# A residual-add RMSNorm on one core: static addresses on SyncE, gamma in 16 chunks on the bulk queue, no block barrier

## The chip, the cores and the metric

The kernel runs on one core of a Trainium2 chip. The metric is the device time of one execution in microseconds (us); lower is better. "Span" is the time from the first to the last instruction in a profile; the device time was 1.7 to 2.1 us longer than the span in every run, and verdicts rest on the device time.

## The reference

```python
batch, seq, dim = 32, 2048, 2048          # x, residual: float32; gamma: float32[2048]; eps 1e-6
z = x + residual
rms = np.sqrt(np.mean(z ** 2, axis=-1, keepdims=True) + eps)
return (z / rms * gamma).astype(np.float32)
```

There are 65,536 rows of 8 KB. Each row of x and of the residual is read once and each output row written once, 1610.6 MB in all.

## The kernel before

The rows are cut into 74 tiles: 128 partitions x 3 rows, then x 5, then 72 tiles of 128 x 7 rows (7.34 MB for each of x, residual and output). SyncE issues every bulk transfer. VectorE adds the residual into x (L179), ScalarE squares and sums (L230) and takes the root (L238), VectorE scales by the reciprocal and gamma (L184). SyncE's turn for tile i stores tile i-1, loads residual i+1 and loads x i+1:

```python
def sp_turn(sp, t):
    i = t.i
    t.wait(sp, "done", -1)
    inc(sp.dma_start(out=t.dram(o_f, o_full, -1), in_=z[(i - 1) % 2][:, : sizes[i - 1], :]), "s_out", i - 1)
    ...
    t.wait(sp, "add_a")
    load_r(sp, t, 1)
    t.wait(sp, "s_out", -1)
    ...
    load_x(sp, t, 1)
```

Turns 3 to 70 stand in a hardware loop whose addresses are worked out in registers:

```python
@block.sync
def _(sp):
    load_x(sp, Turn(0))
    load_r(sp, Turn(0))
    load_r(sp, Turn(1))
    load_x(sp, Turn(1))
    for i in range(1, LO):
        sp_turn(sp, Turn(i))
    with sp.Fori(0, 2 * n_iter, 2) as it:
        for i in range(LO, LO + 2):
            sp_turn(sp, Turn(i, it))
    ...
```

Gamma is read four times, into partitions 0, 32, 64 and 96, by ScalarE's queue; VectorE then copies it to all partitions of a PSUM tile with one shuffle:

```python
@block.scalar
def _(s):
    s.wait_ge(tail_ev["add"], 1)
    for q in range(4):
        s.dma_start(out=r_area[32 * q : 32 * q + 1, R, :], in_=gamma.partition_broadcast(1)).then_inc(g_in, U)
```

Of the kernel before, what the change touches and what calls it, by code (L numbers as in the profile page):

```python
# [9 lines left out]
def kernel(  # L10
# [17 lines left out]
    nc = tc.nc  # L28
    P = nc.NUM_PARTITIONS
# [4 lines left out]
    x_f = x.flatten_outer_dims()  # L34
    r_f = residual.flatten_outer_dims()
    o_f = out.flatten_outer_dims()

    n_rows, D = x_f.shape
    R = 7
    STEP = 4  # L40
    U = 16
    lead = [3, 5]
    n_full = (n_rows // P - sum(lead)) // R
    sizes = lead + [R] * n_full
    starts = [0]
# [3 lines left out]
    n_tiles = len(sizes)  # L49
    last = n_tiles - 1  # L50

    LO = 3
    n_iter = (last - 1 - LO) // 2
    HI = LO + 2 * n_iter
    assert n_iter >= 1

    def rows(t, i):
        k = sizes[i]
        return t[starts[i] : starts[i] + P * k, :].rearrange("(p r) m -> p r m", r=k)

    def full(t):
        return t[starts[2] :, :].rearrange("(n p r) m -> n p r m", p=P, r=R)

    x_full, r_full, o_full = full(x_f), full(r_f), full(o_f)

    inv_d = 1.0 / float(D)

    def sb(name, shape):
        return ctx.enter_context(nc.sbuf_tensor(name, shape, fp32))

    def ps(name, shape):
        return ctx.enter_context(nc.psum_tensor(name, shape, fp32))
# [3 lines left out]
    def sem(name):  # L76
        sems.append(ctx.enter_context(nc.semaphore(name)))
        return sems[-1]
# [3 lines left out]
    z = [sb(f"z{p}", [P, R, D]) for p in range(2)]  # L82
    r_area = sb("r_area", [P, R + STEP, D])
# [8 lines left out]
    gamma_tile = ps("gamma_tile", [P, D])  # L92
# [5 lines left out]
    g_in = sem("g_in")  # L98
    dve = sem("dve_own")
    act = sem("act_own")  # L100
    s_tail = sem("s_tail")
    tail_ev = {k: sem(f"tail_{k}") for k in ("add", "rms", "done")}


# [2 lines left out]
    def entry(i):  # L107
        if i == 0:
            return R + STEP - sizes[0]
        return 0 if i % 2 else STEP  # L110
# [7 lines left out]
    class Turn:  # L118
# [10 lines left out]
        def wait(self, eng, kind, d=0):  # L129
            eng.wait_ge(ev[kind][(self.i + d) % 2], self.at(d))  # L130

        def dram(self, t, t_full, d):
            if self.it is None:
                return rows(t, self.i + d)
            return t_full[self.it + (self.i + d - 2)]

    def inc(ins, kind, i):
        return ins.then_inc(ev[kind][i % 2], U)


    def load_x(sp, t, d=0):
        i = t.i + d
        inc(sp.dma_start(out=z[i % 2][:, : sizes[i], :], in_=t.dram(x_f, x_full, d)), "x_in", i)  # L143

    def load_r(sp, t, d=0):
        i = t.i + d
        e = entry(i)
        inc(
            sp.dma_start(out=r_area[:, e : e + sizes[i], :], in_=t.dram(r_f, r_full, d)),
            "r_in",  # L150
            i,
        )

    def sp_turn(sp, t):
        i = t.i
        t.wait(sp, "done", -1)
        inc(
            sp.dma_start(out=t.dram(o_f, o_full, -1), in_=z[(i - 1) % 2][:, : sizes[i - 1], :]),  # L158
            "s_out",
            i - 1,  # L160
        )
        if t.it is None and i == last:
            return
        t.wait(sp, "add_a")
        load_r(sp, t, 1)
        t.wait(sp, "s_out", -1)
        if t.it is None and i + 1 == last:
            for k, (a, b) in enumerate(tail):
                sp.dma_start(  # L169
                    out=z[last % 2][:, a:b, :], in_=rows(x_f, last)[:, a:b, :]  # L170
                ).then_inc(x_tail[k], U)
        else:
            load_x(sp, t, 1)


    def add(v, i, a, b):
        e = entry(i)
        s = z[i % 2][:, a:b, :]
        return v.tensor_add(out=s, in0=s, in1=r_area[:, e + a : e + b, :])  # L179

    def scale(v, i, a, b, rs, c=0):
        for g in range(a, b):
            s = z[i % 2][:, g, :]
            ins = v.scalar_tensor_tensor(  # L184
                out=s,
                in0=s,
                scalar=rs[:, c + g - a : c + g - a + 1],
                in1=gamma_tile[:, :],
                op0=mult,
                op1=mult,  # L190
            )
        return ins

    def dve_turn(v, t, own):
        i, p = t.i, t.p
        t.wait(v, "x_in")
        t.wait(v, "r_in")
        (a0, b0), (a1, b1) = parts(i)
        inc(add(v, i, a0, b0), "add_a", i)
        inc(add(v, i, a1, b1), "add_b", i)  # L200
        for h, (a, b) in enumerate(parts(i)):
            n = b - a
            t.wait(v, "rms_a" if h == 0 else "rms_b")
            v.reciprocal(out=rstd[p][h][:, :n], in_=rms[p][h][:, :n]).then_inc(dve, U)  # L204
            v.wait_ge(dve, own(i, h))
            ins = scale(v, i, a, b, rstd[p][h])
        inc(ins, "done", i)
# [42 lines left out]
                i,  # L250
            )

    block_ctx = nc.Block()
    block = block_ctx.__enter__()

    @block.sync
    def _(sp):
        load_x(sp, Turn(0))
        load_r(sp, Turn(0))
        load_r(sp, Turn(1))  # L260
        load_x(sp, Turn(1))
        for i in range(1, LO):
            sp_turn(sp, Turn(i))
        with sp.Fori(0, 2 * n_iter, 2) as it:
            for i in range(LO, LO + 2):
                sp_turn(sp, Turn(i, it))
        for i in range(HI, n_tiles):
            sp_turn(sp, Turn(i))
        for k, (a, b) in enumerate(tail):
            sp.wait_ge(tail_ev["done"], k + 1)  # L270
            sp.dma_start(
                out=rows(o_f, last)[:, a:b, :], in_=z[last % 2][:, a:b, :]
            ).then_inc(s_tail, U)
        sp.wait_ge(s_tail, U * len(tail))
        sp.wait_ge(ev["s_out"][(last - 1) % 2], ((last - 1) // 2 + 1) * U)

    @block.vector
    def _(v):
        row = R
        v.memset(eps_tile[:, :], float(eps))  # L280
        v.memset(r_area[:, row, :], 0.0).then_inc(tail_ev["add"], 1)  # L281
        v.wait_ge(g_in, 4 * U)
        v.stream_shuffle(gamma_tile[:, :], r_area[:, row, :], [0] * 32)  # L283
        for i in range(LO):
            dve_turn(v, Turn(i), lambda i, h: (2 * i + h + 1) * U)
        with v.Fori(0, 2 * n_iter, 2) as it:
            for i in range(LO, LO + 2):
                dve_turn(v, Turn(i, it), lambda i, h: it * (2 * U) + (2 * i + h + 1) * U)
        for i in range(HI, last):
            dve_turn(v, Turn(i), lambda i, h: (2 * i + h + 1) * U)  # L290
        base = 2 * last * U
        t = Turn(last)
        t.wait(v, "r_in")

        def tail_scale(k):
            a, b = tail[k]
            v.wait_ge(tail_ev["rms"], k + 1)
            v.reciprocal(out=tail_rstd[:, a:b], in_=tail_rms[:, a:b]).then_inc(dve, U)  # L298
            v.wait_ge(dve, base + (k + 1) * U)
            scale(v, last, a, b, tail_rstd, a).then_inc(tail_ev["done"], 1)  # L300

        for k, (a, b) in enumerate(tail):
            v.wait_ge(x_tail[k], U)
            add(v, last, a, b).then_inc(tail_ev["add"], 1)
            if k:
                tail_scale(k - 1)
        tail_scale(len(tail) - 1)

    @block.scalar
    def _(s):  # L310

        s.wait_ge(tail_ev["add"], 1)
        for q in range(4):
            s.dma_start(
                out=r_area[32 * q : 32 * q + 1, R, :], in_=gamma.partition_broadcast(1)
            ).then_inc(g_in, U)
        chain = Chain(s, act)
        for i in range(LO):
            act_turn(s, Turn(i), chain)
        with s.Fori(0, 2 * n_iter, 2) as it:  # L320
            n = chain.n
            chain.base = it * R
            for i in range(LO, LO + 2):
                act_turn(s, Turn(i, it), chain)
            assert chain.n - n == 2 * R
        chain.base = None
        chain.n = n + 2 * R * n_iter
        for i in range(HI, last):
            act_turn(s, Turn(i), chain)
        for k, (a, b) in enumerate(tail):  # L330
            chain.wait()
            s.wait_ge(tail_ev["add"], k + 2)
            act_part(
                s, chain, z[last % 2], a, b, tail_ssq[:, a:b], tail_rms[:, a:b]
            ).then_inc(tail_ev["rms"], 1)

    block_ctx.__exit__(None, None, None)

    ids = [a.num for a in sems]
    assert ids == list(range(ids[0], ids[0] + len(ids)))  # L340
    nc.gpsimd.sem_clear(range(ids[0], ids[-1] + 1))
# [35 lines left out]
```

## Time and profile before

| | before |
|---|---|
| device time, median of 3, later 4 runs | 3727.06, later 3727.15 us (3726.29 to 3727.42) |
| span of the profiled run | 3724.2 us |
| VectorE, ScalarE busy | 62%, 29% |
| DMA rate over the span | 432 GB/s |

The prediction below shows the lines of the page and of both edges. Two more readings: The first is the timeline around gamma (columns: start, duration, engine, line, operation, out<-in with shapes, count; in brackets the idle time before and what ended it):

```profile
14.70 2.29 DVE L283 STREAM_SHUFFLE gamma_tile<-r_area 128x2048 f32<-128x2048 f32 x1
19.36 4.43 DVE L179 TENSOR_TENSOR z<-z,r_area 128x4096 f32<-128x4096 f32 x1 [2.38 <-DMA r_area<-in_residual_dram]
```

The shuffle is over before the first residual lands, so gamma costs VectorE no waiting.

The second is the DMA view of the steady part alone, 200 to 3600 us (packets, MB and rate; then each queue with its packets, MB and share of 16 engines' time):

```profile
DMA packets 28936, 1474.96 MB, mean 434 GB/s; under 512 B 3215, under 2 KB 3215, under 8 KB 3215
...
q1 hardware_dynamic: 28936, 1474.96, 100.2%
```

Only the bulk queue q1 moves anything here. No gamma packet (queue q10) and no instruction packet (queue q14) falls into this window.

**A reading that needs the packet records.** The trace has the start, duration, size and queue of each DMA packet, but not its engine. A transfer over 16 engines ends with sixteen packets of 4 bytes, one from each engine. Sorting their ends for each transfer gives how far each engine is behind the middle one; I call the largest of these the **lag**.

### The profile page before, as it was taken

The numbers are of one execution on the slowest core, as the hardware profiler recorded it, in microseconds if no ns is written. First come the engines' busy times: TensorE is split into PE (matmuls) and PEld (weight loads), VectorE is DVE, ScalarE is ACT, GpSimd is POOL, SyncE is SP. The second block draws the span as 40 slices with busy tenths as digits, with TensorE's granted clock in tenths as the row PEclk, the third lists the DMA queues.
The fourth block names the chain that finished last, engine by engine and source line by source line (L and its number), as shares of the span: only waits on it lengthen the run. The fifth ranks groups of instructions, "written<-read, shape, count | busy, mean of one in ns | idle before, by whom it ended". The sixth has DMA issues, their size and how long they took to land.

```text
span 3724.2 us, 4147 instructions
## 1 busy us (share of the span) xinstructions
DVE 2302.6 (62%) x816; ACT 1072.4 (29%) x1176; POOL 0.2 (0%) x4
## 2 busy tenths in 40 slices
DVE  4666565566665566665566665566665566665566
ACT  2333322233322233322233322233322233322233
POOL 0000000000000000000000000000000000000000
DMA  9999999999999999999999999999999999999999
GB/s 420 430 434 434 434 434 434 434 434 434 434 434 434 434 434 434 433 434 434 434 434 434 434 434 434 435 434 434 435 434 434 434 435 434 434 434 434 434 434 400
DMA packets 32842, 1610.68 MB, mean 432 GB/s; under 512 B 3652, under 2 KB 3652, under 8 KB 3652
## 3 DMA queue, kind: packets, MB, share of 16 engines
q1 hardware_dynamic: 32832, 1610.63, 100.0%
q10 hardware_dynamic: 8, 0.03, 0.0%
q14 instruction: 2, 0.02, 0.0%
HBM read 1073.77 MB, written 536.87 MB: 432 GB/s over the span
## 4 chain that ended last, share of the span: by engine, by line
DMA 66%; DVE 22%; issue 9%; ACT 2%; SPq 0%; DVEq 0%; ACTq 0%
DMA out_dram<-z 33%; DMA z<-in_x_dram 33%; DVE z L179 15%; DVE z L184 7%; ACT sq_junk L230 1%; DMA r_area<-in_residual_dram 0%; ACT rms L238 0%; DVE rstd L204 0%; SPq L158 0%; DVEq L130 0%; ACTq L218 0%; ACTq L130 0%; DVE tail_rstd L298 0%; SPq L143 0%; SPq L169 0%
## 5 line engine op out<-in xcount | busy, mean ns | idle before, releaser
L179 DVE TENSOR_TENSOR z<-z,r_area 128x8192 f32<-128x8192 f32 (+2 forms) x150 | 1109.4, 7436 | 1257.3 <-DMA z<-in_x_dram 1227.2
L230 ACT ACTIVATE sq_junk<-z 128x2048 f32<-128x2048 f32 x512 | 963.4, 1882 | 2613.5 <-DVE z L179 2602.1
L184 DVE SCALAR_TENSOR_TENSOR z<-z,rstd,gamma_tile 128x2048 f32<-128x2048 f32 x505 | 1153.5, 2343 | 5.2
L204 DVE RECIPROCAL rstd<-rms 128x4 f32<-128x4 f32 (+2 forms) x146 | 25.2, 173 | 130.9 <-ACT rms L238 130.9
L230 ACT ACTIVATION_READ_ACCUMULATOR sq_junk<-z 128x1 f32 x512 | 95.4, 186 | 0.0
L238 ACT ACTIVATE rms<-ssq,eps_tile 128x4 f32<-128x4 f32 (+2 forms) x146 | 43.3, 297 | 13.4
L184 DVE SCALAR_TENSOR_TENSOR z<-z,tail_rstd,gamma_tile 128x2048 f32<-128x2048 f32 x7 | 16.2, 2345 | 0.1
L283 DVE LOAD_MASK_SELECT gamma_tile<-r_area x1 | 0.0, 14 | 11.5 <-DMA r_area<-in_gamma_dram 11.5
L230 ACT ACT_TABLE_LOAD x1 | 1.3, 1283 | 4.7 <-issue 4.7
L283 DVE STREAM_SHUFFLE gamma_tile<-r_area 128x2048 f32<-128x2048 f32 x1 | 2.3, 2290 | 0.0
L281 DVE MEMSET r_area<- 128x2048 f32 x1 | 1.8, 1765 | 0.4 <-issue 0.4
L238 ACT ACT_TABLE_LOAD x1 | 1.3, 1283 | 0.1
L238 ACT ACTIVATE tail_rms<-tail_ssq,eps_tile 128x2 f32<-128x2 f32 (+1 forms) x4 | 1.2, 295 | 0.1
L280 DVE MEMSET eps_tile<- 128x1 f32 x1 | 0.1, 59 | 1.0 <-SPq L80 1.0
L298 DVE RECIPROCAL tail_rstd<-tail_rms 128x2 f32<-128x2 f32 (+1 forms) x4 | 0.6, 157 | 0.0
L358 POOL MEMSET const-bfloat16-1.0<- 128x1 bf16 x1 | 0.1, 102 | 0.0
L358 POOL MEMSET const-uint8-127<- 128x1 uint8 x1 | 0.1, 102 | 0.0
L358 POOL MEMSET const-float32-0.0<- 128x1 f32 x1 | 0.1, 99 | 0.2 <-issue 0.2
L358 POOL MEMSET const-float32-1.0<- 128x1 f32 x1 | 0.1, 99 | 0.0
## 6 DMA issues: line engine op xcount, KB each, us to landing
r_area<-in_residual_dram SPq DMA_DIRECT2D x72, 7168.0 KB, 27.0
z<-in_x_dram SPq DMA_DIRECT2D x71, 7168.0 KB, 33.8
out_dram<-z SPq DMA_DIRECT2D x71, 7168.0 KB, 34.2
z<-in_x_dram SPq DMA_DIRECT2D x3, 2048.0 KB, 26.3
out_dram<-z SPq DMA_DIRECT2D x3, 2048.0 KB, 15.5
r_area<-in_residual_dram SPq DMA_DIRECT2D x1, 5120.0 KB, 29.5
z<-in_x_dram SPq DMA_DIRECT2D x1, 5120.0 KB, 42.6
out_dram<-z SPq DMA_DIRECT2D x1, 5120.0 KB, 25.2
```

Of the source, the lines that this page charges most:

```text
L179: return v.tensor_add(out=s, in0=s, in1=r_area[:, e + a : e + b, :])
L184: ins = v.scalar_tensor_tensor(out=s, in0=s, scalar=rs[:, c + g - a : c + g - a + 1], in1=gamma_tile[:, :], op0=mult, op1=mult,)
L204: v.reciprocal(out=rstd[p][h][:, :n], in_=rms[p][h][:, :n]).then_inc(dve, U)
L230: s.activation(out=sq_junk[:, :], in_=src[:, g, :], func=Act.Square, accum_out=sq[:, g - a : g - a + 1],)
L238: return s.activation(out=rm, in_=sq[:, : b - a], func=Act.Sqrt, bias=eps_tile[:, :], scale=inv_d)
L280: v.memset(eps_tile[:, :], float(eps))
L281: v.memset(r_area[:, row, :], 0.0).then_inc(tail_ev["add"], 1)
L283: v.stream_shuffle(gamma_tile[:, :], r_area[:, row, :], [0] * 32)
L298: v.reciprocal(out=tail_rstd[:, a:b], in_=tail_rms[:, a:b]).then_inc(dve, U)
L358: nc = _bacc.Bacc("TRN2", target_bir_lowering=False, num_devices=1)
```

## The change

Its intent: SyncE's loop is unrolled so that all addresses are constants; gamma is cut so that all 16 DMA engines share it, and goes through the bulk queue in place of a queue of its own; the block with its barrier at the end is replaced by one semaphore. The loops of VectorE and ScalarE stay.

```diff
-    block_ctx = nc.Block()
-    block = block_ctx.__enter__()
-
-    @block.sync
-    def _(sp):
+    stage = r_area[:, 5:7, :].rearrange("p r m -> p (r m)")
+    stage = stage.rearrange("p (a b) -> p a b", a=16)[:, :, : D // 16]
+
+    def sync_program(sp):
         load_x(sp, Turn(0))
         load_r(sp, Turn(0))
+        sp.wait_ge(tail_ev["add"], 1)
+        for q in range(4):
+            sp.dma_start(
+                out=stage[32 * q : 32 * q + 1],
+                in_=gamma.partition_broadcast(1).rearrange("p (a b) -> p a b", a=16),
+            ).then_inc(g_in, U)
         load_r(sp, Turn(1))
         load_x(sp, Turn(1))
-        for i in range(1, LO):
-            sp_turn(sp, Turn(i))
-        with sp.Fori(0, 2 * n_iter, 2) as it:
-            for i in range(LO, LO + 2):
-                sp_turn(sp, Turn(i, it))
-        for i in range(HI, n_tiles):
+        for i in range(1, n_tiles):
             sp_turn(sp, Turn(i))
...
         sp.wait_ge(ev["s_out"][(last - 1) % 2], ((last - 1) // 2 + 1) * U)
+        sp.sem_inc(fin, 1)
...
-        v.memset(r_area[:, row, :], 0.0).then_inc(tail_ev["add"], 1)
+        v.memset(stage, 0.0).then_inc(tail_ev["add"], 1)
...
-        s.wait_ge(tail_ev["add"], 1)
-        for q in range(4):
-            s.dma_start(
-                out=r_area[32 * q : 32 * q + 1, R, :], in_=gamma.partition_broadcast(1)
-            ).then_inc(g_in, U)
...
-    block_ctx.__exit__(None, None, None)
+    sync_program(nc.sync)
+    vector_program(nc.vector)
+    scalar_program(nc.scalar)
+    nc.gpsimd.wait_ge(fin, 1)
```

(The helper that chose between static and register addresses went too; the destination of gamma leaves gaps, 128 elements used of each 256, so that the 16 chunks stay apart.)

More of the change, by code (lines that the diff above doesn't have):

```diff
@@ L59, in rows @@
         return t[starts[i] : starts[i] + P * k, :].rearrange("(p r) m -> p r m", r=k)
-    def full(t):
-        return t[starts[2] :, :].rearrange("(n p r) m -> n p r m", p=P, r=R)
-    x_full, r_full, o_full = full(x_f), full(r_f), full(o_f)
     inv_d = 1.0 / float(D)
@@ L101 @@
     s_tail = sem("s_tail")
+    fin = sem("fin")
     tail_ev = {k: sem(f"tail_{k}") for k in ("add", "rms", "done")}
@@ L130, in wait @@
             eng.wait_ge(ev[kind][(self.i + d) % 2], self.at(d))
-        def dram(self, t, t_full, d):
-            if self.it is None:
-                return rows(t, self.i + d)
-            return t_full[self.it + (self.i + d - 2)]
     def inc(ins, kind, i):
@@ L142, in load_x @@
         i = t.i + d
-        inc(sp.dma_start(out=z[i % 2][:, : sizes[i], :], in_=t.dram(x_f, x_full, d)), "x_in", i)
+        inc(sp.dma_start(out=z[i % 2][:, : sizes[i], :], in_=rows(x_f, i)), "x_in", i)
     def load_r(sp, t, d=0):
@@ L148, in load_r @@
         inc(
-            sp.dma_start(out=r_area[:, e : e + sizes[i], :], in_=t.dram(r_f, r_full, d)),
+            sp.dma_start(out=r_area[:, e : e + sizes[i], :], in_=rows(r_f, i)),
             "r_in",
@@ L157, in sp_turn @@
         inc(
-            sp.dma_start(out=t.dram(o_f, o_full, -1), in_=z[(i - 1) % 2][:, : sizes[i - 1], :]),
+            sp.dma_start(out=rows(o_f, i - 1), in_=z[(i - 1) % 2][:, : sizes[i - 1], :]),
             "s_out",
@@ L161, in sp_turn @@
         )
-        if t.it is None and i == last:
+        if i == last:
             return
@@ L166, in sp_turn @@
         t.wait(sp, "s_out", -1)
-        if t.it is None and i + 1 == last:
+        if i + 1 == last:
             for k, (a, b) in enumerate(tail):
@@ L275, in _, with vector_program @@
         sp.wait_ge(ev["s_out"][(last - 1) % 2], ((last - 1) // 2 + 1) * U)
-    @block.vector
-    def _(v):
-        row = R
+        sp.sem_inc(fin, 1)
+    def vector_program(v):
         v.memset(eps_tile[:, :], float(eps))
-        v.memset(r_area[:, row, :], 0.0).then_inc(tail_ev["add"], 1)
+        v.memset(stage, 0.0).then_inc(tail_ev["add"], 1)
         v.wait_ge(g_in, 4 * U)
-        v.stream_shuffle(gamma_tile[:, :], r_area[:, row, :], [0] * 32)
+        v.stream_shuffle(gamma_tile[:, :].rearrange("p (a b) -> p a b", a=16), stage, [0] * 32)
         for i in range(LO):
@@ L307, in _, with scalar_program @@
         tail_scale(len(tail) - 1)
-    @block.scalar
-    def _(s):
-        s.wait_ge(tail_ev["add"], 1)
-        for q in range(4):
-            s.dma_start(
-                out=r_area[32 * q : 32 * q + 1, R, :], in_=gamma.partition_broadcast(1)
-            ).then_inc(g_in, U)
+    def scalar_program(s):
         chain = Chain(s, act)
```

## The prediction

> **What bounds the kernel now.** I read the page first: busy shares, the row of slices, the DMA queues. No compute engine is near its limit, while the DMA row is full in every slice.
>
> ```profile
> span 3724.2 us, 4147 instructions
> DVE 2302.6 (62%) x816; ACT 1072.4 (29%) x1176; POOL 0.2 (0%) x4
> ...
> DMA  9999999999999999999999999999999999999999
> GB/s 420 430 434 434 434 434 434 434 434 434 434 434 434 434 434 434 433 434 434 434 434 434 434 434 434 435 434 434 435 434 434 434 435 434 434 434 434 434 434 400
> DMA packets 32842, 1610.68 MB, mean 432 GB/s; under 512 B 3652, under 2 KB 3652, under 8 KB 3652
> ...
> q1 hardware_dynamic: 32832, 1610.63, 100.0%
> q10 hardware_dynamic: 8, 0.03, 0.0%
> q14 instruction: 2, 0.02, 0.0%
> ```
>
> The reader is to see that only the first two slices and the last are below 434 GB/s. The bytes are fixed (x and residual in, output out), so at that rate they cost 1610.68 MB / 0.434 = 3711 us. All the rest of the span is 13 us, 0.35%. A change that moves no fewer bytes cannot reach 2%.
>
> Then I asked whether the queue on SyncE could run dry. The table of DMA issues gives the time from issue to landing:
>
> ```profile
> r_area<-in_residual_dram SPq DMA_DIRECT2D x72, 7168.0 KB, 27.0
> z<-in_x_dram SPq DMA_DIRECT2D x71, 7168.0 KB, 33.8
> out_dram<-z SPq DMA_DIRECT2D x71, 7168.0 KB, 34.2
> ```
>
> One such transfer alone takes 7.34 MB / 434 GB/s = 16.9 us. So a residual load stands about 10 us in the queue behind other work, the other two kinds about 17 us. SyncE could issue each of them 10 us later without an engine falling idle; fewer instructions per issue cannot help in the steady part.
>
> Last, the windows of busy time over both edges of the span, where the missing 13 us must be (columns: window and its length, DVE, ACT and POOL busy, clock, DMA share, GB/s):
>
> ```profile
> 0.00:1.00 1.00, 0.00 (x0) 0.00 (x0) 0.20 (x4) 1.00 0.00 0
> 1.00:2.00 1.00, 0.58 (x2) 0.00 (x0) 0.00 (x0) 1.00 0.47 98
> ...
> 3714.00:3716.00 2.00, 0.00 (x0) 0.00 (x0) 0.00 (x0) 1.00 0.92 393
> 3716.00:3718.00 2.00, 0.00 (x0) 0.00 (x0) 0.00 (x0) 1.00 0.84 356
> 3718.00:3720.00 2.00, 0.00 (x0) 0.00 (x0) 0.00 (x0) 1.00 0.30 127
> 3720.00:3721.00 1.00, 0.00 (x0) 0.00 (x0) 0.00 (x0) 1.00 0.12 49
> 3721.00:3722.00 1.00, 0.00 (x0) 0.00 (x0) 0.00 (x0) 1.00 0.12 49
> 3722.00:3723.00 1.00, 0.00 (x0) 0.00 (x0) 0.00 (x0) 1.00 0.00 0
> ```
>
> The first data packet starts 2.0 us after the first instruction. At the end a DMA share of 0.12 is two engines of 16: fourteen have finished and two still work. In the packet records the sixteen engines end between 3717.13 and 3722.27 us, with the last two at 3721.72 and 3722.27; all had equal bytes on the bulk queue. The kernel ends with its **slowest DMA engine**, and 1.9 us of barriers follow it.
>
> From the same records I followed how far each engine's completion of a transfer comes behind the middle of the sixteen. At the second transfer (the residual of tile 0) one engine is 1.31 us late, the next 0.66. The late one carries gamma: 4 packets of 8192 B at 309 ns and 4 of 9 ns, 1.27 us of its own work. By 130 us the latest engine is 3.94 behind; it then stays at 3.77 to the end, probably the same one. Another engine starts ahead of the middle but loses a little all the time (some 2.7 ns in each packet of 57344 B), passes 3.77 at about 3400 us and ends 4.0 to 4.1 behind. In this execution that **drifting engine**, not gamma's, ends last, by 0.55 us.
>
> **What the Trainium skill says.** The page "DMA: Bandwidth & Descriptors", section "Where 436 GB/s comes from", puts the ceiling at 435.2 GB/s; the trace agrees with 434. Its section "Issuing engines are not separate DMA queues" says that transfers issued from different engines interleave on the same 16 DMA engines; the trace agrees, gamma's packets on q10 stand between bulk packets of one engine from 7.4 to 14.2 us. Its section "Why a DMA increments its semaphore by 16 and not by 1" says that a DMA spreads over the largest number of engines up to 16 that divides the slowest dimension of both patterns; the trace shows 8 packets on q10 for four gamma reads, so one data packet and one semaphore packet each, one engine. The page "Runtime: NRT & Kernel Launch", section "Instruction fetch mechanics", says that instructions are streamed through a DMA queue of the sequencer; here q14 carried two packets of 8192 B inside the span, 0.31 us of one engine each.
>
> **The change, part by part.**
>
> 1. *Gamma in 16 chunks on the bulk queue.* The four reads leave ScalarE for SyncE, each cut into 16 pieces of 512 B, by the rule above one for each engine. Packets of 8192 and 16384 B take 309 and 611 ns, so 7 ns plus 36.9 ns per KB; 512 B is about 26 ns. Each engine then carries 4 x (26 + 9) = 0.14 us more, and gamma's former engine 1.27 less 0.14 = 1.13 us less. On the path this is +0.14 us where the drifting engine ends last, and up to -1.13 us where gamma's engine would.
>
> 2. *The order at the start.* On the bulk ring gamma now stands behind x and residual of tile 0. SyncE waits for the memset (ends at 3.24 us), issues four small reads at some 0.3 us, then the loads of tile 1 by about 5.5 us instead of 2.3. The first two transfers keep the engines until 17 us, so nothing runs dry. Gamma reaches VectorE at about 18.8 us rather than 14.7; the shuffle of 2.29 us then comes before the first add instead of beside the load. The first add goes from 19.36 to about 21 us and the first store's issue from 36.99 to about 38.7. The transfers of tile 1 occupy even the fastest engine until 41.8 us. So 3 us of room is left and the cost is nil.
>
> 3. *Static addresses.* A dynamic issue costs SyncE about 0.17 us more (from 120.43 to 120.60 us in the trace), all of it beside 10 us of queue: zero. The listing of instructions grows from 43 to 232 rows on SyncE, 12 KB at the page's 64 B per instruction (estimate; 16 KiB holds 256), so one to three more packets of 0.31 us on q14, each on one engine of sixteen: an expected +0.04 us on the last one.
>
> 4. *No block barrier.* At the start one branch before the first issue goes: -0.05 us. At the end, from SyncE's wake at 3722.74 to the start of the semaphore clear at 3723.09 lie 0.35 us of gathering and releasing; one increment and one wait replace it, about 0.15 us by the hops in the same stretch (0.03 to 0.08 each): -0.2 us.
>
> Sum with the drifting engine last: 0.14 + 0.04 - 0.05 - 0.2 = about -0.1 us. With gamma's engine last: -1.13 in place of +0.14, so about -1.3 us.
>
> **The rivals.**
>
> *The whole lag of gamma's engine comes back.* For it: this engine is the latest of the sixteen for the first 3400 us, and not every execution need have the drifting one. The profiled execution took 3726.27 us where the median of three was 3727.06, so executions differ by as much as is at stake here. Against it: in the trace the drifting engine ends later and owes nothing to gamma; taking gamma away uncovers it at once. It would make 3725.7 us.
>
> *Gamma behind the bulk becomes a new wait.* The shuffle delays the first store, and if the ring runs dry, all engines idle. Against it is the room of 3 us in part 2. If gamma's small reads took 3 us longer than I think, it would cost about 1 us: 3728.
>
> *The straight-line SyncE program stalls on its instruction fetch.* Under a full ring a fetch waits behind packets of 2.1 us; for: two fetches seen. Against: an issue may be 10 us late unnoticed. It would make a change of less than 0.3 us.
>
> *The steady lag is caused by register addresses.* If the drift of one engine came from the dynamic form, static addresses would stop it, and together with gamma's change the end would come about 2 us earlier: 3725. I see nothing in the packet records that ties an engine to SyncE's registers, so I give this one chance in ten.
>
> **Range and chances.** I give 0.55 to -0.1, 0.3 to -1.3, 0.1 to -2, and 0.05 to +1, each from 3727.06: the mean is -0.6 us, so 3726.4. The three runs before span 0.95 us, and lags of engines of 1 to 4 us arise in the first 130 us in bursts which I can't foresee. A range from 3724.6 to 3728.0 should hold it 8 times in 10. Two per cent is 75 us, six times all that is not transfer at full rate: 0.99 within, 0.005 for each side.
>
> **What would show it right or wrong.** In the profile after, q10 should be gone and q1 should have 4 x 32 = 128 packets more; the completion of the residual of tile 0 should have its latest engine 0.6 to 0.7 us behind the middle instead of 1.31; the first add should start near 21 us, the first store be issued near 38.7, with the DMA row still full around 42 us. The steady slices should stay at 434 GB/s and the waits of SyncE be unchanged in kind. The tail from the last packet to the end should be 0.2 us shorter than 1.9. The prediction is wrong if steady slices rise above 435 or fall below 433, if a slice near the start shows a hole, or if the two trailing engines at the end are gone, in which case the gain is near 2 us.

## The result, and the profile after

| | before | after |
|---|---|---|
| device time, median of 4 runs | 3727.15 us (3726.29 to 3727.42) | 3726.23 us (3726.21 to 3726.45) |
| span of the profiled run | 3724.2 us | 3724.7 us |
| ratio of the runs | | 0.9998, 95% interval 0.9981 to 1.0015 |

A ratio is the mean time of one kernel's runs over that of the other's runs of the same rounds, so it is not quite the ratio of the medians quoted. Its interval is 6 us to either side, so it says nothing about effects of 1 us; for those I look at whether the single runs of two kernels overlap.

The page of the changed kernel:

```profile
span 3724.7 us, 3652 instructions
...
GB/s 420 432 434 434 434 434 434 432 434 434 435 434 434 434 434 436 434 434 434 433 434 434 434 434 434 434 434 434 434 434 434 434 434 434 434 434 434 434 434 398
DMA packets 32964, 1610.69 MB, mean 432 GB/s; under 512 B 3712, under 2 KB 3776, under 8 KB 3776
...
q1 hardware_dynamic: 32960, 1610.66, 99.9%
q14 instruction: 4, 0.03, 0.0%
...
r_area<-in_residual_dram SPq DMA_DIRECT2D x72, 7168.0 KB, 27.2
z<-in_x_dram SPq DMA_DIRECT2D x71, 7168.0 KB, 33.8
out_dram<-z SPq DMA_DIRECT2D x71, 7168.0 KB, 34.5
```

The steady rate (434 GB/s over 200 to 3600 us in both) and the times to landing of the bulk transfers are unchanged within 0.3 us. q10 is gone, and q1 has 32960 - 32832 = 128 packets more: four reads of 16 data and 16 semaphore packets, so gamma is spread over 16 engines as intended. q14 carries four packets instead of two. In the steady window (DMA view, 200 to 3600 us) they are new:

```profile
q1 hardware_dynamic: 28926, 1474.56, 100.2%
q14 instruction: 2, 0.02, 0.0%
```

The start, from the timeline:

```profile
3.26 2.51 SPq L255 DMA_DIRECT2D r_area<-in_gamma_dram  x4
5.81 0.58 SPq L140 DMA_DIRECT2D r_area<-in_residual_dram  x1
6.44 0.43 SPq L134 DMA_DIRECT2D z<-in_x_dram  x1
19.64 2.29 DVE L276 STREAM_SHUFFLE gamma_tile<-r_area 128x2048 f32<-128x2048 f32 x1
...
39.46 0.35 SPq L149 DMA_DIRECT2D out_dram<-z  x1
```

A gamma read takes SyncE 0.63 us to issue. The shuffle now stands in front of the first add, and the first store goes out at 39.46 us instead of 36.99.

Both edges of the span (the same columns as in the prediction):

```profile
1.00:2.00 1.00, 0.59 (x2) 1.00 (x1) 0.00 (x0) 1.00 0.34 74
...
3716.00:3718.00 2.00, 0.00 (x0) 0.00 (x0) 0.00 (x0) 1.00 0.58 246
3718.00:3720.00 2.00, 0.00 (x0) 0.00 (x0) 0.00 (x0) 1.00 0.19 82
3720.00:3721.00 1.00, 0.00 (x0) 0.00 (x0) 0.00 (x0) 1.00 0.08 33
3721.00:3722.00 1.00, 0.00 (x0) 0.00 (x0) 0.00 (x0) 1.00 0.06 25
3722.00:3723.00 1.00, 0.00 (x0) 0.00 (x0) 0.00 (x0) 1.00 0.06 25
```

A share of 0.06 is one engine of 16. The share falls earlier than before (0.58 instead of 0.84 from 3716 to 3718 us), so most engines finish earlier; but one works alone from 3720.2 us on, and its last packet ends at 3723.08 us instead of 3722.27. At the last load of a whole tile (near 3649 us, where the sixteen ends of two transfers don't mix) the mean of the engines is 0.7 us earlier than before, and the lag 5.72 us instead of 4.19. So the engines on average gained and the last one lost. This is what the experiments have to explain: **did the parts do nothing, or did they cancel?**

### The profile page after: what moved, and what is told of

Same layout as the page of the kernel before. It is cut to its first block, busy times and chain, and to the rows that moved or that the text cites. A ratio compares the mean times of both kernels' runs of the same rounds, so it can differ in the third digit from the quotient of the medians. Undisturbed runs are those within 1.5% of the kernel's fastest.

```text
span 3724.7 us, 3652 instructions
## 1 busy us (share of the span) xinstructions
DVE 2302.5 (62%) x816; ACT 1072.4 (29%) x1176; POOL 0.2 (0%) x4
## 3 DMA queue, kind: packets, MB, share of 16 engines
q1 hardware_dynamic: 32960, 1610.66, 99.9%
## 4 chain that ended last, share of the span: by engine, by line
DMA 66%; DVE 22%; issue 9%; ACT 2%; SPq 0%; DVEq 0%; ACTq 0%
DMA out_dram<-z 33%; DMA z<-in_x_dram 33%; DVE z L170 15%; DVE z L175 7%; ACT sq_junk L221 1%; DMA r_area<-in_gamma_dram 0%; ACT rms L229 0%; DVE rstd L195 0%; DVEq L126 0%; SPq L255 0%; DVE r_area L274 0%; ACTq L209 0%; ACTq L126 0%; DVE tail_rstd L291 0%; SPq L160 0%
```

## The experiments

My theory at the start was that of the prediction: one drifting DMA engine ends last and owes nothing to gamma, so no part moves the time by more than 0.3 us. The rivals: gamma's part really gains about 1 us; static addresses gain or lose; the barrier is the gain. All twelve kernels gave correct outputs. Times, with the kernel before in the same rounds on the same chip:

| run | median (range), us | before in the same rounds |
|---|---|---|
| gamma only | 3725.67 (3725.29 to 3725.70) | 3726.67 (3726.30 to 3727.69) |
| static only | 3727.63 (3727.32 to 3728.17) | the same |
| no barrier only | 3726.67 (3726.50 to 3726.77) | the same |
| after, gamma in one packet | 3727.19 (3726.91 to 3729.95) | the same |
| 56 reads, one engine | 3748.72 (3748.51 to 3749.00) | 3726.53 (3726.47 to 3730.28) |
| 56 reads, all engines | 3750.00 (3749.75 to 3750.18) | the same |
| gamma behind the second residual | 3738.21 (3738.09 to 3738.41) | the same |
| gamma before the first residual | 3726.70 (3726.14 to 3726.93) | the same |
| the changed kernel again | 3726.57 (3726.29 to 3726.80) | 3726.61 (3725.88 to 3727.91) |
| gamma and no barrier, dynamic loop | 3725.29 (3725.19 to 3725.49) | the same |
| changed kernel, more SyncE code | 3727.69 (3727.48 to 3727.86) | the same |
| one read of 59 rows, one engine | 3735.93 (3735.81 to 3736.08) | the same |

### The three parts one by one

**Gamma only.** The kernel before with the lines of the diff that concern gamma, `stage` and the memset; loop and block stay.

> The kernel before with one part of the change: gamma in 16 chunks of 512 B on SyncE's bulk queue; the dynamic loop and the block barrier stay. My theory (the drifting DMA engine sets the end, not the one that carried gamma): the residual of tile 0 has its latest engine 0.6 to 0.7 us behind the middle instead of 1.31, but the time stays that of before within 0.4 us, 3726.7 to 3727.5. Rival (the lag of gamma's engine comes back in full in executions without a profile's luck): 0.8 to 1.2 us faster than before, about 3726.1, so this part alone makes the 0.9 us seen.

Measured: 1.0 us faster at the median, and its slowest run is below the fastest of before. My theory falls, the rival's number holds. The residual of tile 1 has a lag of 0.54 us instead of 1.34 in the records.

**Static only.**

```diff
-        for i in range(1, LO):
-            sp_turn(sp, Turn(i))
-        with sp.Fori(0, 2 * n_iter, 2) as it:
-            for i in range(LO, LO + 2):
-                sp_turn(sp, Turn(i, it))
-        for i in range(HI, n_tiles):
+        for i in range(1, n_tiles):
             sp_turn(sp, Turn(i))
```

> The kernel before with SyncE's loop unrolled to static addresses only. My theory: nothing, 3726.7 to 3727.5, since each issue has 10 us of queue ahead; one to two more instruction packets of 0.31 us. Rival (register addresses cause the drift of one engine): the drift of about 1.3 to 1.5 ns per us is gone in the records and the time is about 1 us lower. The change's own profile still drifts, which speaks against it already.

Measured: 1.0 us slower at the median; one run of before reaches into its range. Both expectations fail. The slow drift of one engine is still there, so register addresses are not its cause, and something in the unrolled program costs time.

**No barrier only.** The block removed, the three programs called one after the other, `fin` as in the diff.

> The kernel before without the block and its barrier, nothing else. My theory: from the last packet to the last instruction 1.6 us instead of 1.9, so 0.3 us faster than before, about 3726.8. Rival (the barrier is the whole 0.9 us): 3726.2. Second rival (nothing at all, the 0.9 us is spread between executions): 3727.1.

Measured: the same median as before. In the records the tail from the last packet to the last instruction is 1.59 us instead of 1.90, as expected, but the time doesn't show it in these five runs.

So the parts are about -1.0, +1.0 and 0 us: they cancel.

The record also lists the span of every run, and this splits the numbers further. The device time exceeds the span by 2.1 us in before and in "static only", and by 1.8 us in "gamma only", "no barrier only" and the changed kernel (2.07 to 2.14 and 1.74 to 1.82 us in the single runs). So of the 1.0 us of "gamma only" 0.7 us lie within the span (median 3723.9 where before has 3724.6) and 0.3 us outside it. "No barrier only" has the same 0.3 us outside, and yet its span is 0.3 us longer (3724.9), although its tail is 0.3 us shorter: its stream ended later, and that ate up both. "Static only" loses its 0.9 us within the span (3725.5). The traces don't show what lies outside the span, so the 0.3 us stay unexplained, and only the 0.7 us of gamma's part can be put down to the DMA engines.

### Where the unrolled program loses

The q14 packets of the steady part are the suspect. In the changed kernel they start at 1135.17 and 3304.80 us, 309 and 312 ns long and 8192 B each. SyncE had then started 79 and 207 instructions, exactly 128 apart, in the static-only run too (1212.11 and 3370.97 us). 8192 B / 128 is 64 B for each instruction: they are refills of SyncE's program. In each case a bulk packet of 57344 B starts 3 or 4 ns ahead of the end of the refill, and takes 2532 and 2534 ns instead of 2116. A refill thus costs one engine 0.31 + 0.41 = 0.72 us (in "static only" 0.61 and 0.72). The lags around them, worked out from the records of the changed kernel (us behind the middle, the five latest engines, sorted):

```
transfer ends at 1128.20:  0.63  1.44  1.53  1.90  2.62
transfer ends at 1145.14:  1.34  1.44  1.53  1.90  2.62     after the refill at 1135
transfer ends at 3293.96:  1.42  1.52  1.94  2.88  4.51
transfer ends at 3310.87:  1.42  1.52  1.94  2.88  5.25     after the refill at 3305
```

Both times one engine jumps by 0.71 to 0.74 us, and the engine at 0.63 is the one that drifts on to 4.51: it is the only one whose lag grows steadily between. The refills hit the very engine that ends last.

Two runs test this. **The changed kernel with its static addresses taken back** (gamma in chunks and no barrier on the dynamic loop of before):

> The changed kernel without its static addresses: gamma chunked, no barrier, the dynamic loop of before. Theory (the two instruction refills of the unrolled SyncE program cost the last engine 0.7 us each): no q14 packet after 200 us, 0.7 to 1.3 us faster than the changed kernel, 3725.3 to 3725.8, so better than both. Rival (static addresses cost nothing where gamma is chunked): the time of the changed kernel.

Measured: 1.3 us faster than the changed kernel on the same chip, without overlap of their runs, and faster than every run of before. The device time exceeds the span by 1.8 us in both, so all of it lies within the span. Its DMA view of 200 to 3600 us has no q14 line:

```profile
DMA packets 28930, 1474.79 MB, mean 434 GB/s; under 512 B 3212, under 2 KB 3212, under 8 KB 3212
...
q1 hardware_dynamic: 28930, 1474.79, 100.2%
```

**The changed kernel with more code on SyncE**:

```diff
         t.wait(sp, "s_out", -1)
+        for _ in range(4):
+            sp.sem_inc(junk, 1)
         if i + 1 == last:
```

> The changed kernel with 4 more semaphore increments (on a semaphore nobody waits for) in each of SyncE's turns: 535 instructions instead of 247. Refills came at SyncE's 79th and 207th instruction, 128 apart, so here also at the 335th and 463rd: four q14 packets after 200 us instead of two. Theory: each makes one engine, the one that ends last, 0.72 us later, so 1.4 us slower than the changed kernel. Rival (refills are hidden): no change; SyncE itself has 10 us to spare for each issue.

Measured: 1.12 us slower than the changed kernel, without overlap. The same view, with four refills (at 508, 1424, 2354 and 3304 us):

```profile
q1 hardware_dynamic: 28918, 1474.10, 100.1%
q14 instruction: 4, 0.03, 0.0%
```

With 0, 2 and 4 refills on one chip the medians are 3725.29, 3726.57 and 3727.69 us: 0.64 and 0.56 us for each. In the records all four hit the engine that ends last. The rival (refills are hidden) falls. That a refill costs a little less time than its 0.72 us of lag I can't explain further.

**The changed kernel again**, on the chip of these two:

> The changed kernel itself once more, so that it stands beside the next runs on one chip. In three chips' runs the kernel before had medians of 3726.5 to 3727.2. Theory (gamma's part gains 1 us, the longer SyncE program gives most of it back, the barrier is worth nothing measurable): 3726.2 to 3726.7, up to 0.6 us faster than before. Rival (the changed kernel is really 0.9 us faster, as in its first runs): 3725.6 to 3726.0 where before has 3726.6.

Measured: 0.04 us below before at the median, as the theory expected; the rival falls. The 0.9 us between the medians of the first four runs each did not come again; the runs of before spread over 2 us on this chip, those of the changed kernel over 0.5.

### Where gamma's part gains

**Gamma in one packet, but behind the bulk.** The changed kernel with `out=r_area[32 * q : 32 * q + 1, 5, :], in_=gamma.partition_broadcast(1)` in place of the chunks.

> The changed kernel with gamma again as one packet of 8192 B a quarter on one engine, still issued by SyncE behind the residual of tile 0. My theory (drift sets the end): that engine is 1.1 to 1.3 us later after the start, the time is that of the changed kernel within 0.4 us, 3725.9 to 3726.7. Rival (gamma's lag sets the end): 0.9 to 1.2 us slower than the changed kernel, about 3727.2.

Measured: 3727.19 us against 3726.57 for the changed kernel, on another chip (before had 3726.67 and 3726.61 there), so about 0.6 us slower (1.0 against the first runs of the changed kernel); my theory's range, up to 3726.7, fails, and the rival's 3727.2 holds. Two of its five runs were 2 us slower still. The profiled one is one of these: packets of all engines are stretched by 2 us an engine between 3340 and 3440 us, which I saw in no other kernel at that size. Once before had a run as slow, 3730.28, without a profile. The first store is issued at 39.39 us, as late as in the changed kernel, so the later start is not what gains.

**Gamma before the first residual.** The changed kernel with `load_r(sp, Turn(0))` moved behind the four gamma reads.

> The changed kernel with gamma's reads before the residual of tile 0, behind x of tile 0 only. Gamma lands near 11 us, the shuffle is hidden again, the first add starts near 19.5 us instead of 21.8 and the first store comes 2 us earlier. Theory (that room is not needed): the time of the changed kernel within 0.4 us, 3725.9 to 3726.7. Rival (the later first store of the changed kernel costs something at the start): 0.5 us or more faster than the changed kernel.

Measured: 3726.70 us where before has 3726.53; nothing is gained by the earlier first store (36.76 us), and the rival's 0.5 us don't come. (The changed kernel didn't run on this chip, and the next table has more stretch here than in it: a small gain of the earlier store could be hidden by that.)

What the records show, in all runs in which the ring (SyncE's queue of issued transfers) never ran dry, is one relation. The table has the lag of the residual of tile 1 and the stretch of all packets that start 38 to 150 us after the first packet, divided by 16 engines:

| kernel | lag, us | stretch for each engine, us |
|---|---|---|
| changed kernel with more SyncE code | 0.43 | 0.32 |
| gamma only | 0.54 | 0.39 |
| changed kernel (two profiles) | 0.64, 0.76 | 0.58, 0.54 |
| gamma and no barrier | 0.65 | 0.35 |
| gamma before the first residual | 0.85 | 1.37 |
| after, gamma in one packet | 1.27 | 1.75 |
| before | 1.34 | 2.07 |
| static only, no barrier only | 1.34, 1.38 | 2.20, 2.45 |

Where one engine is late in the first transfers, packets of the **other** engines are longer too, at the changes from loading to storing: in before those of all sixteen near 40 and 128 us, of about ten near 82 us. (Each packet starts 3 or 4 ns before the last one of its engine ends, so the engines can be told apart over such a stretch.) Gamma in whole packets makes such a late engine, by the 1.27 us of the prediction. Taking this away saves 2.07 - 0.39 = 1.7 us of stretch at the start, of which part is lost later: at the transfer near 317 us the mean of the engines is 1.0 us earlier in "gamma only" than in before, at the last whole tile 0.6, which agrees with the 0.7 us gained within the span.

This is a relation, and not yet a cause. In the three runs with a long dry ring (56 reads, twice, and "gamma behind the second residual", below) the engines start level again, the latest 0.32 to 0.38 us behind the middle at the first store, and the same window still has 2.0 to 2.1 us of stretch. So a late engine is not the only thing that lengthens packets. And "gamma before the first residual" has 0.8 us more stretch than the changed kernel at nearly the same time.

**One engine made later on purpose.** My first try added 56 reads of 4 KB on ScalarE's queue to the kernel before, each in one packet:

```diff
+        for q in range(56):
+            s.dma_start(
+                out=scr[q : q + 1, :], in_=gamma.partition_broadcast(1)[:, :1024]
+            ).then_inc(g_x, U)
```

> The kernel before with 56 more reads of 4 KB (gamma's first half again, into a scratch tile that nothing reads), each one packet on the engine that carries gamma: by the packets' fit 56 x (158 + 9) ns = 9.4 us of more work for that one engine in the first 100 us, 0.23 MB in all. Theory A (an early lag of one engine is never made up, the engine that comes last sets the end): that engine ends 3.8 + 9.4 = 13 us behind the middle, in place of the drifting one at 4, so 9 us slower, 3735 to 3737. Theory B (the queue of 10 to 17 us ahead of each issue evens the engines out before the end): within 1 us of before, 3726 to 3728.

The other half of the pair had the same reads cut into 16 chunks:

> The same 56 reads, cut into 16 chunks of 256 B, so that each of the 16 engines gets one chunk of each: 56 x (16 + 9) ns = 1.4 us for every engine. Theory A: 1.4 us slower than before, about 3728.5, a seventh of the cost of the same bytes on one engine. Theory B: within 1 us of before as well.

Measured: 22 and 23 us slower, far outside both theories. The pair failed as an experiment. The timeline of the first shows why (ACTq is ScalarE's queue):

```profile
4.67 42.68 ACTq L322 DMA_DIRECT2D scr<-in_gamma_dram  x56
```

The 56 issues kept ScalarE's program for 42.68 us, 0.76 us each, so the squares of tile 0 started at 48.98 us instead of 23.82, the first store went out at 62.15 and the ring ran dry. What it does show: a dry ring lets all engines start level again (lag 0.38 us at the first store), and yet at the last load of a whole tile the last engine was again 5.1 us behind the middle. The spread at the end is not a memory of the start alone.

The repair is a single issue of 59 rows, which has no divisor up to 16 and so ran on one engine (68 packets on q10: 8 for gamma, 59 rows and one semaphore):

```diff
+        s.dma_start(
+            out=scr[:59, :], in_=gamma.partition_broadcast(59)[:, :1024]
+        ).then_inc(g_x, U)
```

> A repair of the earlier try, whose 56 issues kept ScalarE from its squares and so emptied the ring: the kernel before with a single read of 59 rows of 4 KB into a scratch tile. 59 has no divisor up to 16, so it should run on one engine, 59 x 0.158 = 9.3 us of work more for that engine. Theory A (a lag of one engine is carried to the end): it ends some 13 us behind the middle and the time is 8 to 9.5 us longer, 3735 to 3736. Theory B (engines even out): within 1 us of before. If the read is spread over all engines instead, the cost is 0.6 us.

Measured: 9.3 us slower. Theory A's time holds, but not its picture. At the last load of a whole tile the last engine is only 6.2 us behind the middle, not 13. The mean of all engines is 8.3 us later than in before by 140 us and stays so: one engine's 9.3 us of extra work have become everybody's by then, partly as idle time, partly as 4.4 us of stretch for each engine (with a lag of 3.74). The windows of busy time:

```profile
40.00:60.00 20.00, 11.49 (x4) 2.83 (x4) 0.00 (x0) 1.00 0.93 377
...
100.00:120.00 20.00, 18.23 (x8) 14.61 (x16) 0.00 (x0) 1.00 0.89 373
...
3728.00:3730.00 2.00, 0.00 (x0) 0.00 (x0) 0.00 (x0) 1.00 0.14 57
```

Every turn of SyncE waits for whole transfers, all 16 engines, so a late engine holds up the issues that the others live on. In gamma's case the ring never ran dry, and why packets stretch there I can't say from these runs. That the stretch is what costs the time in gamma's case is argued from the table, not shown by a run of its own.

### Was the order at the start free?

**Gamma one place further back**: the changed kernel with `load_r(sp, Turn(1))` moved ahead of the gamma reads.

> The changed kernel with gamma's four reads one place further back, behind the residual of tile 1 too. Gamma then lands 12 us later, the first add starts near 34 us and the first store is issued near 51.5, while the loads of tile 1 end at 41 to 42. Theory (the order was free only because the first store still came before the ring ran dry, with some 1.8 us of room): all engines idle from about 42 to 52 us and the time is 10 us longer, 3735 to 3737.5. Rival (the start is hidden behind the stream whatever its order): the time of the changed kernel, 3726 to 3727.

Measured: 11.7 us slower than before in the same rounds, 0.7 us above the range of the theory. The windows of busy time:

```profile
40.00:45.00 5.00, 1.32 (x3) 4.88 (x7) 0.00 (x0) 1.00 0.31 131
45.00:50.00 5.00, 4.90 (x4) 1.34 (x3) 0.00 (x0) 1.00 0.00 0
50.00:55.00 5.00, 5.00 (x3) 1.12 (x1) 0.00 (x0) 1.00 0.56 236
```

The DMA share is 0 from 45 to 50 us, because the first store was issued at 51.62 us. The rival (the start is hidden whatever its order) falls. Gamma landed 12 us later than in the changed kernel (31.80 instead of 19.64 us), and the first store went out 12 us later too. The room of the changed kernel is only about 2 us of these: its first store is issued at 39.46 us, and its fastest engine finished loading tile 1 at 41.7. That would make a hole of 10 us; I can't account for the other 1.7.

## Why the prediction was right or wrong

The number was right: 3726.4 predicted, 3726.23 and in the repetition 3726.57 measured. Its working was right in the bound and wrong in two terms that cancelled, so that the number came out this close is in part luck. (The weights given make -0.6 us from 3727.06, that is 3726.5; the text has 3726.4.)

- **The bound.** Right. Over 200 to 3600 us the rate stayed at 434 GB/s, and the times to landing of the bulk transfers moved by at most 0.3 us. What moved lies in the first 1000 us, in the refills and at the end. Two of the prediction's signs of being wrong came all the same, without meaning what they were to mean. Single slices of the page read 432 and 436 GB/s after, outside its 433 to 435, while the mean didn't move. And the two trailing engines became one, which ends 2.9 us after the next (3723.08 and 3720.19 us), without the gain of 2 us.
- **Gamma's part ("+0.14 us where the drifting engine ends last").** Wrong, and the step that failed is "taking gamma away uncovers it at once": I took an early lag to be one engine's own affair. The records show longer packets on all engines where one is late early, and with gamma spread the mean of the sixteen ends 0.6 us earlier, so the drifting one gained as well. The term is -1.0 us ("gamma only"), 0.7 of it within the span; why the packets stretch stays open.
- **The rival "the whole lag of gamma's engine comes back".** Its amount, -1.13, is close to the 1.0 measured, but not its way: the lag of the trailing engines at the end doesn't come from gamma, it is as large with gamma spread (4.19 us before, 4.38 in "gamma only", at the last load of a whole tile).
- **The order at the start.** Right that it costs nothing. The sizes were off: an issue of gamma took 0.63 us, not 0.3; the first add started at 21.84 and the first store at 39.46 us instead of 21 and 38.7; so the room was about 2 us and not 3. The working had the fastest engine busy with tile 1 until 41.8 us; the packet records of before have 42.2. "Gamma behind the second residual" shows that an order which goes beyond this room costs.
- **Static addresses ("an expected +0.04 us on the last one").** Wrong. The number of refills in the steady part, two, is within the one to three said. The size of one was 0.31 and measured 0.72 us, because the next bulk packet on the engine is slower as well. And the chance of 1 in 16 was no chance: both hit the engine that ends last, in the changed kernel and in "static only", and so did all four in "more SyncE code". The term is +1.0 to +1.3 us.
- **The barrier.** -0.2 us predicted; the tail in the records went from 1.90 to 1.59 us. The time of "no barrier only" is that of before all the same, since its stream ended later.
- **The rival of register addresses.** It falls. One engine's lag grew by 1.32 ns per us before and by 1.47 in the changed kernel (between 1872 and 3090 us, without a refill). What makes it drift stays open; so does why it is the one that the refills use.

The sum of what was measured, -1.0 + 1.0 to 1.3 + 0, is 0.0 to +0.3 us. The repetition gave -0.04, the first comparison -0.9, with runs of before that spread over 1 to 2 us.

The better kernel is neither of the two: gamma's chunks without the barrier, on the old dynamic loop, at 3725.29 us, 1.3 us or 0.035% below both on its chip.

## What to carry to other kernels

When a kernel is bound by its DMA engines, look at each engine and not at their mean: a small transfer on one engine, or a program refill, costs a single engine time, and here the kernel ended when the last engine did. Spread even an 8 KB constant over all engines if it is read while the stream starts, and don't unroll an issuing engine's loop that has slack anyway, for its longer program comes through the same engines. A change with several parts that measures as nothing should be taken apart before it is believed to be nothing.

## What the Trainium skill lacked or had wrong

- "Runtime: NRT & Kernel Launch", section "Instruction fetch mechanics", speaks of refills in blocks of 16 KiB (256 instructions), mostly hidden, and of full unrolling as what kernels prefer. Here SyncE's refills were packets of 8192 B, 128 instructions apart, each took 0.72 us (once 0.61) of one DMA engine, and the unrolled loop was 1.0 us (alone) and 1.3 us (with the other parts) slower. The page looks at the sequencer; this cost fell on a DMA engine.
- "DMA: Bandwidth & Descriptors", section "Where 436 GB/s comes from", says that for transfers between HBM and SBUF the HBM side (about 358 GB/s) binds. Taken by itself this is wrong for a core that runs alone: this one held 434 GB/s in such transfers from 200 to 3600 us. The page's own table of measurements, just above, has 425 GB/s for one core and keeps 358 for two cores that stream at once; the sentence lacks that condition.
- The same page, section "Issuing engines are not separate DMA queues", calls the sequencer's time for an issue usually small relative to the DMA. For small reads it was not: 56 issues from ScalarE took 0.76 us each, where the data packet of each took 0.16 us, and they cost the kernel 22 us.
- No page says what a few small packets on one engine do to a full stream at its start: the kernel with gamma's four reads of 8 KB cut and on the bulk queue was 1.0 us faster, with 1.7 us less stretch in the mean of the engines.
- "DMA: Bandwidth & Descriptors", section "Latency and other measured facts", says that engines 7 and 15 are usually slower than the others in traces, as something of transfers issued by GpSimd, and gives no size. All transfers here were issued by SyncE and ScalarE, the trace doesn't number the engines, and one of them still lost 1.3 to 1.5 ns per us, and at the last load of a whole tile the last engine was 3.5 to 6.1 us behind the mean of the sixteen.
